# A two-layer attention trunk on one core: 464 instructions change places in a written-out order

## The chip, the cores and the metric

The kernel runs on one core of a Trainium2 chip. The time is that of the core on the device, in microseconds (us), from one execution to the next. A core has a matrix engine (TensorE, in the profile PE, with its weight loads as PEld), a vector engine (VectorE, DVE), a scalar engine (ScalarE, ACT), a general one (GpSimd, POOL) and a queue engine (SyncE, SP) that here issues nearly all DMA transfers. Each engine works through its own list of instructions in order, and waits at an instruction until what it needs is there.

## The reference, cut to what matters

Two layers over 1024 tokens of width 1024, with 256 context tokens; layer 0 is grouped-query attention with rotary positions, layer 1 neighbourhood attention with a bias. Both have a SiLU gate path, adaLN modulation ahead of the projection, and a gated residual.

```python
for i in range(DEPTH):                       # DEPTH = 2
    mod_x = (silu_c @ w_mod[i] + b_mod[i])[:, None, :]
    mod_c = silu_cc @ w_mod[i] + b_mod[i]
    hx = rms_norm(x, norm_g[i]) * (1.0 + sc_x) + sh_x
    hc = rms_norm(ctx, norm_g[i]) * (1.0 + sc_c) + sh_c
    if i % N_MIXERS == 0:
        yx, yc = gqa_axial_mixer(hx, hc, ...)      # 16 query heads, 4 key heads, 1280 keys
    else:
        yx, yc = neighbourhood_mixer(hx, hc, ...)  # 16 heads, 8 x 16 window and 256 context keys
    x = x + g_x * yx
    if not last:
        ctx = ctx + g_c * yc
return rms_norm(x, final_norm_g)
```

## The kernel before

The work is tiled by 128 tokens: 8 tiles of x, 2 of context. Matrices are multiplied as pairs of float16 parts (a high part and the rest), three matmuls for each product. The program has these stages:

- **Start** (0 to about 50 us). `mod_cols` computes the modulation of layer 0 from `w_m0`: for each of eight blocks kt two loads `wm{kt}0` and `wm{kt}1` (L780, 512 KB each), 16 matmuls into `pm` (L787), a copy `mrow` (L789) and small matmuls (L796) whose results become the scales `acol` and `scol`. `ln_pre` loads a tile of x into `xstage` (L1046, 512 KB), squares it on ACT (`xj`, L1049), takes the root (`ms_ln` L840 on DVE, `rs_ln` L842, a power on POOL), and scales it (L1052). `h_kt` transposes the scaled tile on PE into `pl` (L1061), from which ACT makes x's high part (L1066) and DVE the rest (L1068, L1071). `load_w` brings weights of the keys and values (`wskv`, L1026, 256 KB) and splits them (ACT L912, DVE L913). `kv_mm` multiplies (`pkv`, L1075). Ahead of all, 26 matmuls named `idle` (L1023) run on a tile of ones.
- **Layer 0** (about 50 to 700 us). For each of eight pairs of heads: projections `pa` (L1224), norms and rotary positions of the queries (DVE L986, L995), scores `st` (L1474), exponentials `pf` and `ph` (ACT L1461, L1459), the split of the probabilities (POOL L1326), products with the values `pv` (L1332 to L1336), and the eviction to `og` (ACT L1308, DVE L1310 to L1314). A part of the scores is computed in the other orientation (`qs`, `qpf`, `qpp`, `qpv`).
- **The seam** (about 700 to 765 us). The output projection `poa` and the residual (`x`, L1577 on POOL), the norm of layer 1 (`lss` L855, `ms_ln`, `rs_ln`, L859, L860), its split into `hrb` (ACT L871, DVE L872), and the first projections of layer 1.
- **Layer 1** (to the end). The projections of a pair of heads u, queries and keys in `b_qk`, values and gate in `b_vz`, are one Winograd-Strassen product each (`winograd`): seven block products (PE L1739 into `pwq{u}a` to `d`, L1787 into `pwv{u}a` to `d`) and sums on DVE (L1681 to L1700) between them. `b_load` loads weights into `wsb` (L1646), forms sums of them in `wtb` (POOL L1649 to L1651), and splits both into `wb` (ACT L1653, DVE L1654). `put_v` evicts values to `bv` (ACT L1768, DVE L1769), `put` evicts keys and queries to `bk` and `bq` (ACT L1726 to L1730, DVE L1727, L1731). Attention follows as in layer 0: scores `bsn` and `bsc` (L1820, L1821), maxima `bmx` and `bnx` (DVE L1839 to L1850), exponentials `bph` and `bpf` (ACT L1858 to L1861), transposes by DMA (L1864), values `bpv`. Last come the output projection `pob` (L1959) and the final norm.

What sets the order: the code above is first recorded in the order in which it is written. Then a table of numbers, `TABLE`, gives for each engine, ACT, DVE, PE, POOL and SP in turn, the order in which its recorded instructions are to stand: each entry is the step, less one, from the position of one instruction in the recording to that of the next. `settle` reads the table and `apply` lays it on the program. So each engine's list is an order written out by hand or by a search; at run time nothing is reordered. The waits between engines follow from the data, and from which buffer is reused: `bank`s of PSUM of each tag come in twos, so that the third user of a tag waits for the eviction of the first.

Where the new order puts a matmul later, it also puts its weight load (PEld) later. Where a step of `load_w` or `b_load` is moved, the loads that SP issues for it are rows of their own and may keep their place.

Of the kernel before, what the change touches and what calls it, by code (L numbers as in the profile page):

```python
# [61 lines left out]
y<TM?;?Uj`ke_eEIM4r(c9!O}n7Ew^`oV(p51ra716@KMo$P+=V@8?W-MX0ReVGo2!tQgy&C%5ApQASn2!F+z*T3J(z=)3mX?~?ARjZrTyMqjN<=r-
wkl_udfOGsQdA6c5Ioq9cBt?m#}T_=DCTT^FNpm;Bu`)xi8GPVLdEzWxG1I;8;hZZC!0*-}WO1Q_wS`t;;n7x@-KfvwcUqT-XlnJ7#X*a4NX51@kx856
szu#dXczI;S9R25~lQiPk}luN&kR*akD@96q-
7ctP1QGuLy@nog(<9TN!OR8iU0)`ib?LUS+{L@7&M*qCfP3a53X>h1Pi%gz>WSKDUjI$?W5f4e+7Hgo%I*QQy@_POr$Gq*2%bbpYb1H_T44;Q}g!GiKz
Q53VFw|1!isH|%X4II{e%nz4t|Hd;rsn<IMr9Ia>Th0Yj+vk7K&V{}Y93FlNpW}6l*vr;chYmIjLTX0OoKBcq=<1x)o*afy1iEnqw_)3M;s0mOPWZP%$
# [2013 lines left out]
```

## Time and profile before

| | us |
|---|---|
| three runs | 1301.15, 1302.62, 1303.58 |
| their median | 1302.62 |
| the profiled execution | 1301.96 |
| its span, first to last instruction | 1300.2 |

The page of the profile gives busy time by engine; the table of waits gives for each engine what it waited for and how long; the windows cut the span into stretches; the timeline shows single instructions as start, duration, engine, line, operation, output and inputs, with the idle time before it in brackets and what ended it. Line numbers are those of the kernel before.

### The profile page before, as it was taken

To read this page: it belongs to the slowest core of one execution; us is meant where nothing else is said; L and a number is where in the kernel's file an instruction comes from. 1 tells how busy PE (TensorE), PEld (TensorE's weight loads), DVE (VectorE), ACT (ScalarE), POOL (GpSimd) and SP (SyncE) were. 2 spreads that over 40 slices of the span, in tenths; PEclk is the share of its full clock that TensorE was granted. 3 is DMA by queue.
4 is the path that set the end of the run, shared out by engine and by line. 5 is a ranking of instruction groups with operands and counts; after the bars stand their busy time and mean duration, and the time that the engine had idled before them with its cause. 6 is when DMAs were issued, how large, how long until landed. Compare 5 with 4: busy or idle time off the path is not lost. (4 is left out here: it accounts for less than half of the span.)

```text
span 1300.2 us, 36307 instructions
## 1 busy us (share of the span) xinstructions
PE 1277.7 (98%) x13597; PEld 908.6 (70%) x13597; DVE 1049.0 (81%) x2625; ACT 1015.0 (78%) x2246; POOL 929.2 (71%) x1303
## 2 busy tenths in 40 slices
...
GB/s 364 217 153 84 120 140 148 156 180 155 157 170 156 168 157 148 132 180 188 101 114 192 218 124 87 145 157 143 146 148 158 142 154 147 157 151 204 315 149 113
DMA packets 446016, 209.32 MB, mean 161 GB/s; under 512 B 403280, under 2 KB 409616, under 8 KB 445840
## 3 DMA queue, kind: packets, MB, share of 16 engines
...
q8 instruction: 106, 1.74, 0.5%
...
## 5 line engine op out<-in xcount | busy, mean ns | idle before, releaser
L1326 POOL TENSOR_TENSOR pl<-pf,ph 128x256 f16<-128x256 f32 x322 | 222.7, 713 | 31.5 <-ACT pf L1461 25.4
L1326 POOL TENSOR_TENSOR bph<-bpf,bph 128x256 f16<-128x256 f32 (+1 forms) x224 | 181.2, 825 | 71.0 <-ACT bpf L1860 51.4
L1224 PE MATMUL pa<-wa,x 128*128 128x256 f16 x1536 | 228.3, 272 | 0.4 <-DVE q L1004 0.4
L1326 POOL TENSOR_TENSOR qpp<-qpf,qpp 128x256 f16<-128x256 f32 (+1 forms) x254 | 149.2, 607 | 40.3 <-ACT qpf L1416 29.2
L1787 PEld LDWEIGHTS <-hx 128*128 128x128 f16 x2688 | 162.4, 98 | 11.1 <-issue 3.7
L1224 PEld LDWEIGHTS <-x 128*128 128x128 f16 x1536 | 141.2, 97 | 35.3 <-issue 1.2
L1459 ACT ACTIVATE ph<-st 128x512 f16<-128x512 f32 x190 | 112.0, 598 | 26.5 <-PE st L1475 23.0
L1461 ACT ACTIVATE pf<-st 128x512 f32<-128x512 f32 x190 | 113.3, 603 | 0.5 <-POOL pl L1326 0.3
L1403 DVE CUSTOM_DVE_ANT_0 qpf<-qs,zero 128x512 f32<-128x512 f32 x156 | 92.8, 596 | 23.7 <-POOL qpp L1326 16.6
L1739 PEld LDWEIGHTS <-wb 128*128 128x128 f16 x672 | 63.0, 98 | 66.7 <-issue 2.3
L1415 ACT ACTIVATE qpp<-qpf,qnx 128x512 f16<-128x512 f32 x156 | 101.1, 654 | 9.1 <-DVE pa L990 1.7
L1259 DVE TENSOR_REDUCE mxp<-pm 128x1 f32<-128x512 f32 x152 | 101.5, 682 | 5.6 <-PE pm L1258 5.1
L1336 PE MATMUL pv<-v,pl 128*128 128x65 f16 x760 | 104.9, 193 | 0.0
L1416 ACT ACTIVATE qpf<-qpf,qnx 128x512 f32<-128x512 f32 x156 | 101.9, 653 | 1.9
L1858 ACT ACTIVATE bph<-bpf,bnx 128x384 f16<-128x384 f32 (+1 forms) x128 | 72.4, 584 | 32.7 <-DVE bnx L1850 24.5
L1332 PE MATMUL pv<-v,ph 128*128 128x130 f16 x570 | 89.3, 220 | 0.4 <-DVE og L1314 0.4
L1336 PEld LDWEIGHTS <-pl 128*128 128x128 f16 x760 | 70.5, 97 | 17.1 <-POOL pl L1326 1.6
L1959 PE MATMUL pob<-wob,obf 128*128 128x512 f16 x336 | 81.6, 379 | 0.0
L1649 POOL TENSOR_TENSOR wtb<-wsb 128x256 f32<-128x256 f32 x64 | 56.7, 886 | 25.5 <-DVE wb L1654 11.2
L1336 PE MATMUL bpv<-bv,bpht 128*128 128x65 f16 x608 | 74.8, 192 | 0.0
L1860 ACT ACTIVATE bpf<-bpf,bnx 128x384 f32<-128x384 f32 (+1 forms) x128 | 73.8, 583 | 0.6
L1474 PE MATMUL st<-q,k 128*128 128x512 f16 x190 | 71.1, 379 | 1.0 <-ACT pf L1461 0.8
...
## 6 DMA issues: line engine op xcount, KB each, us to landing
...
```

Source lines behind the costliest of these rows:

```text
L1224: T.matmul(ps[:, :, i, :], hA(a, kt, t), wt[w][:, kt, :], start=n == 0, stop=n == 3 * KT - 1)
L1259: V.tensor_reduce(mxs[i][:, t, ch:ch + 1], pm, axis=AX.X, op=ALU.max)
L1326: G.tensor_tensor(lo[:, c], p32[:, c], hi[:, c], op=ALU.subtract)
L1332: T.matmul(pv[:, c:c + 130], hi, v[:, 0:130], start=first, stop=False)
L1336: T.matmul(pv[:, c:c + 65], lo, v[:, 0:65], start=False, stop=last)
L1403: V.tensor_tensor_reduce(pf.rearrange("p a b -> p (a b)")[:, 0:n], st[:, 0:n], zero.broadcast_to([P, n]), op0=ALU.add, op1=ALU.max, scale=1.0,
L1415: S.activation(ph, pf, AF.Exp, bias=nmx)
L1416: S.activation(pf, pf, AF.Exp, bias=nmx, accum_out=sums[:, t, c:c + 1])
L1459: S.activation(ph, st, AF.Exp)
L1461: S.activation(p32, st, AF.Exp)
L1787: T.matmul(ps[:, t * P:(t + 1) * P], hx[a][:, t, blk, kt], wt[j][:, s_, w, kt], start=first and t == 0 and m == 0, stop=last and t == 3 an ...
L1959: T.matmul(ps, ob[kt][:, t, a], wout["b"][hf][b][:, kt, :], start=n == 0, stop=n == 3 * len(kts) - 1)
```

## The change

Only `TABLE` is another; every instruction and every wait's reason stays. Its first lines, cut:

```diff
-c-qBW31D1R)jn^TeKIrI*CuJ3wzQN2vO|kdz@jVyWm6DE1rbC9LHR{cT)<y`WJmoGl!Aclh%73IKou%2Ev1Dv-
...
+c-
+qZ;2Y_Q`wg0&#J(FZ6(`R<d?(8m$y9)wRcabVQDbhhfo+zLKN)eSO(k$SUM=zo%>Pi!kB2ttlMPa3Hf$ckOr|q;%GU>VB|D5mMo7|Sn48nW=J0;1zUp@
...
```

The new table takes two more lines of text, so each line of the code behind it has a number higher by two (L1769 becomes L1771). Counted as the fewest instructions that have to be taken out and put elsewhere to turn one order into the other, 100 of 13,261 matmuls, 154 of 2,625 operations on DVE, 98 on ACT, 52 on POOL and 60 of the loads and stores of SP change places, 464 together. Most go past one to four neighbours. Three places follow.

**DVE, values of pair 6** (trace: 1115.7 to 1120.6 us). `bv16` is the pair's values, `pwv6a` the first bank of their product, `wb700` the weights of the pair after it, `bq20` its queries. Before:

```order
L1848 TENSOR_REDUCE bnx506_20918<-bmx506_20868 128x2
L1654 SCALAR_TENSOR_TENSOR wb700_20790<-wsb701_20949,wb700_20790 128x3x128
L1850 TENSOR_SCALAR bnx506_20918<-bnx506_20918 128x1
L1727 SCALAR_TENSOR_TENSOR bq20_13049<-c12q6_20665,bq16_20274 64x4x128
L1769 TENSOR_TENSOR bv16_20276<-pwv6a_20673,bv16_20276 128x4x2x64
L1654 SCALAR_TENSOR_TENSOR wb700_20790<-wsb702_21077,wb700_20790 128x3x128
```

Now:

```order
L1850 TENSOR_REDUCE bnx506_20918<-bmx506_20868 128x2
L1656 SCALAR_TENSOR_TENSOR wb700_20790<-wsb701_20949,wb700_20790 128x3x128
L1771 TENSOR_TENSOR bv16_20276<-pwv6a_20673,bv16_20276 128x4x2x64
L1852 TENSOR_SCALAR bnx506_20918<-bnx506_20918 128x1
L1729 SCALAR_TENSOR_TENSOR bq20_13049<-c12q6_20665,bq16_20274 64x4x128
L1656 SCALAR_TENSOR_TENSOR wb700_20790<-wsb702_21077,wb700_20790 128x3x128
```

The subtraction of the values goes ahead of a small operation and of the product for the queries. On ACT the cast of `bv16` (L1768) goes at the same place ahead of the conversion of `wsb702` (L1653).

**PE, values of pair 0** (trace: 757 to 761 us). `wb011` is the weights, half made when the first two of these matmuls run; `pwq0b` is a bank of the product for the queries. Before:

```order
L1787 MATMUL pwv0d_13984<-wb011_13880,hx0_13039 128x128
L1787 LDWEIGHTS hx1_13040
L1787 MATMUL pwv0d_13984<-wb011_13880,hx1_13040 128x128
L1787 LDWEIGHTS hx0_13039
L1787 MATMUL pwv0d_13984<-wb011_13880,hx0_13039 128x128
L1739 LDWEIGHTS wb001_13597
L1739 MATMUL pwq0b_13755<-hx0_13039,wb001_13597 128x512
```

Now the third `pwv0d` stands nearer the end of the `pwq0b` group:

```order
L1741 MATMUL pwq0b_13755<-hx1_13040,wb001_13597 128x512
L1789 LDWEIGHTS hx0_13039
L1789 MATMUL pwv0d_13984<-wb011_13880,hx0_13039 128x128
L1741 LDWEIGHTS wb001_13597
L1741 MATMUL pwq0b_13755<-hx0_13039,wb001_13597 128x512
```

The third matmul into `pwv0d` has moved behind eight of the twelve into `pwq0b`. Beside it, ACT converts `wsb012` (L1653) directly ahead of `wtb011`, and POOL takes the power of the norm (L842) ahead of two sums of weights (L1649, L1651). DVE's rows ahead of the one for `wtb011` (L1654) change only among themselves.

**SP, the start** (trace: 0 to 20 us). The first twelve loads. Before:

```order
L780 DMA wm00_185<-in_w_m0 128x1024
L1046 DMA xstage0_105<-in_x 128x1024
L1026 DMA wskv0_189<-in_a_wkv 128x512
L780 DMA wm01_187<-in_w_m0 128x1024
L1046 DMA xstage1_106<-in_x 128x1024
L780 DMA wm10_202<-in_w_m0 128x1024
L780 DMA wm11_204<-in_w_m0 128x1024
L1046 DMA xstage2_107<-in_x 128x1024
L1046 DMA xstage3_108<-in_x 128x1024
L780 DMA wm20_282<-in_w_m0 128x1024
L1026 DMA wskv1_206<-in_a_wkv 128x512
L780 DMA wm21_284<-in_w_m0 128x1024
```

Now:

```order
L782 DMA wm00_185<-in_w_m0 128x1024
L1028 DMA wskv0_189<-in_a_wkv 128x512
L1048 DMA xstage0_105<-in_x 128x1024
L782 DMA wm01_187<-in_w_m0 128x1024
L782 DMA wm10_202<-in_w_m0 128x1024
L1048 DMA xstage1_106<-in_x 128x1024
L1048 DMA xstage2_107<-in_x 128x1024
L782 DMA wm11_204<-in_w_m0 128x1024
L782 DMA wm20_282<-in_w_m0 128x1024
L1048 DMA xstage3_108<-in_x 128x1024
L782 DMA wm21_284<-in_w_m0 128x1024
L1028 DMA wskv1_206<-in_a_wkv 128x512
```

Weights go ahead of tiles of x at two places, `xstage2` comes ahead of `wm11`, and `wskv1` goes behind `wm21`.

Two swaps more that the prediction speaks of: on DVE the queries' product L995 goes ahead of the eviction L1314 of `og22` (trace: 326.6 us), and on ACT an exponential into `pf` (L1461) goes ahead of one into `ph` (L1459) at 324 us. From 1195 us on, a dozen loads for the output projection (`obf`, `acc`, `wsob`, `fg`) and of the bias table `tb` change places in SP's list; PE's order of the last 60 us is the same in both.

More of the change, by code (lines that the diff above doesn't have):

```diff
@@ L62 @@
[L62 to L66, printed above, removed]
@@ new lines @@
+C80>Cbr5-h57R3xeWL;q71?hU;lQu5B%3ZDb)Y;I!%{<V=o#4onGB^-
+fP(0C(1%5^5&|*_X=rtA^x^C*#ctGPSLUQWm?yDS9$Q7OCL%f_EI5lTie>5{fI5RFH<MLsK}6p=MXsl~V*6M~9W`5?Q6WI~v15Wu?HhAVj<aYG1P8_V{
+B7^}SRWY!z^D0#(IXW$XKKMuIyROej8YCXMq-D{kx>yY#rH-0rQl#G3vVq!{R3O=MkJ!JTp`d0B$I2U22aN+p>)BY1N-
+BOw~kqPw7`K~&_pHyE!SBVN0+foVnXyE8N=uaI=f=w?Q%vqVXOrrF;?jmsICcjb~Zk&);aQ4l-
+u<!CI4AWnKrs8&2vR3}H=5`xpRQouJJ^ix6a7`m>UD<}HXk<sdOWCEv!G$o1(Rq^~-)Rk8>0vcwOn3nQ_(mEjL3X<f?r9DU@l-
+68IXqpz>Q#dgJ2^g6~Vu2<Vg3lYv$s|ox>BtC9%ST=Lr#<P~NkJl^4s5Ff7-|B&D-
@@ new lines @@
+$OZ*F2i2QmQAz<3bpR`mcp`qtSmXsDE`~Zp)GlpKf0dOa64n6DZl(HMqAXKZUe`y>|Bdz|-325)fVVUUqM9I}S$@d<l>A-
+cKHylu!@@ZzH&>dv*7Bm#x`9kqDsPzq29{K)4ysPA^^`ocAF%xd_n+OrQWg^|j&rWQ~9rf23|?*_xJW_i!wT`rX|L{&d0j{_<%*p~NJF)2T4P>qm$v&A
+kEw)!}-
+1o6A>?bA`wx?1HRB4AkBodbbnmhf%CH?>8dWjMa?6`sI10Wk=|>J?s0GpxfL3?(XmI{+{y8Ezj&5jfJwVuipyeZ9RzP&%f@nlTO}>l{>cA;gm^}tEN!@
+QF{>%2p)H=dokVv?}zPN-
+4A;e(jUNXYXI`g4=DU|?Ky8iUdl%&(Qu*4r}vmZ$e*eoMy1V?AsDWQj=>aE#hV8dRMLc87?~H6`+|uYj5koI1tY)_c;JAROK=sWv}+=oapzGvUHL?9hW
+wa|;EanvP-fcinh-*06q5iRsQ?8Rf|~%kvD{S6SR<qbZywMHde9W7d=hqoz9N+L4>ZRSR`BwI)V9GbK%3G_Zaa|R-
@@ new lines @@
+tvNLB*bDkMEo_E206qgii6mD&y<&fe72z=Gm9Y+>ea1i+9>ZG)LX|qwQK-THBd8~EAHZo3oJL?4{}KXtNhOL`0Dg`CzoOTI>ZkGba{xQ>rCKXPs1TB?;
+lP(+PhVL!zKoAozOvH!;cNJ}FU;-
+|%x^3oMW?5R|IhkXT8h9^pI2X>J%Zd`()R=$s?8nXiDOBUD8PmLR?LHkP6iBvA3POr{1HwA70cqa>dRCL3!@=;lmHfxga-
+0N9Pq<?U49SV3%e0BA=guYahs|QWam(Mv8y<WRc%}&sE8jiPMdB)R)-PO2>xk&*EBuZ<l>{ry$zp*$-
+x$~sKmJG2yE^muCyjglk0(Y91OpX`pYQ*AHXg+L4dXJDSq=0{QqeWK-V7I$7&XHH2*8Sb2h-
++d!QbJ_`;s+_KQK)6v_}zW1zLKF%8*JEySmu)p|LoF<!f~7PcYM1R#{r+72XD02l7tYGB%LH4*wH|9=)NDJ(b%-
+&|Yx5V~X(+@@|6S<0H><Z9q&0N?#N75uK5rz$5d*4|$SJo>=?C=rAVF<*bjzaOG$q^u=YyG6VGb(&`&5#@A~>G#%e(fu2>X2lb<g7@PvzK8rh9^d~7N&
@@ new lines @@
+MRj9GeJ4pd|l;;G2iKI2hc^(K!JuhCfr<H>I_+8@vb0-{-JFNNe}@MTb~)0T<jB;hyRI2lGc-NEL;v0Tyi}YHkT#h}NJ^d(c;8kFFEjb;iA;-
+B=1YUzh`lI5Pw{e2=SG)t%qOI-?Jq_S!L`#ssLp;si9fS8C+=n^yY`>KUnhP47H-
+^b&mcJlRTk21nSu19e5X1HNfA5jVm`+JH33gN6=U5Tn}X9pE)Vr*FY6--eq>21(Wta}c8D4gekhks)}@^@f2COW`PZHp>~X@@X!%n`oe|CSv`Mg?OZWy
+Z+{j+NYWtD$p@VJp=K1ikjUzAKq(6*`j#0et65mO;|*R{o#F0oYg4_=fRzzTK4}&>-l4`G;z^pENMoRbk^_fd>#(LmqvuD^}6+*(vxk5x-
+n8Mu?1Nh;U@KK_vq9*?H-
+l0gu>8uc#nP(M8sF*Vq+XB?fKSV=lz!1H|mwqhM~N4?)&$WY1bHmLtMBCNxvAiF1>UU&?`Oi77Y}IKO`o3G>gjtehPpg_?f73-
@@ new lines @@
+m5*E*tc^3)j+&7Q%Xz;xTnuhC+e8;9n?XkpmG3is;~<6yaESTqeVhG)ZIZxn+SH40!ZutvQ73LQZ>Mzy{lpK`E6NID}J43>U587__?D2^jpL^QT4h)j(
+SKB~`kli*LmL-
+@XMjqi_ic>xJk7(3pxmu#OQT63MD!x0hX~n~IC!w|rvW^Wir9_)UxowCg;|M93)Df6%?qHLGBg4mlCq{{lyS)*Y&WAWc|!_HRT>_;@@8a<Jrps;7;UI7
+o=Vrf7o}4{P|mMW3PO|C^!z5bf4_1GfJrMO;40-
+J(0X7;Y%xef|0h=&^D)CnRkXKv4G`3nkH({QgXQz2~gADS+q|l+h9hdj8PoKWCCDGWbaMyaYF>wkbLqg)wr+wFsQAxsrtbD*VwQ?N@$ajhdvwH}AakXA
+)fUX8;W{c;Q?M&t*g<y1_aDG|86vqOJI~Uw`e_>Zl}LY%<a*e^kXsy@{pNF@B07dhgq4=ihHu`z2F^-
+5viZ!b0_047BF5aMQwVTq3ZFUx))GD@B7NKAQadqi|e=2)`UoanPv;;NdU9UzN4Gny4??VNr*cqH3Bc6GrL42};Zpp8Cwcc-
@@ new lines @@
+CaT}aZM*8?BH3^9jbDbvUr}2WG@Fa)#C;^K%xK_Lh=*9OJFSl^<yYMekG<0R3f69CCi>99D@eql4usi}U9i%0STKbEX(U!b<;v*+=Fx0ab#=VqmpHKJS
+nMcsreEm)j!qU2n`Kx~fzChjG8#tP~2=Buuy}Xx(tX@2r%gQglfvEB@E$Q{-
+ao1l8e>wqfJBORef1)RB{SSKZUss_Mz6I@X%TeSzMKyi!^K&WI7&aQUpM4*0B}u;a5<ZOIz_)pp=f?tEe$AD9Tq}<V#4pv&Ga(lc_gsx2pR!`RuZ90U?
+_}8h3jO&JB8j}~+rgh`dB&92rEbFd>ie*aPublGk`5gZ%53A3x(~cXDp<OXTuWK7wXjaN#^5rs{iTBdUVwwAt3X|-
+c=<pg(P7UWR&*mtEU4~kDCMpUUM9&=K<Sej1lRCwaCwxVVZA4AY$U!-X2zu#-
+W*S_V&F9E#Tt7#^9_|{v_PYZRCLsUyr>}UIT_N^V5%M9*SPuf1cWQ}`H`=NQd)HB+NGuYt9g27xb(AhxZE#3HMUqaW&bfu%X~#9oPSEtbapEv=4+^-
@@ new lines @@
+hSGjG<SIrni#9GY&cZ72q;InBTzFJVJN;&VEn8!Z3bp3tmsBGSd#|SbAwn^VrImiY>;d`+(7s5I9Y=HTgsmcqc1iPo@qk#WK#Cz-c%P#sYn3&-
+uPwUBB<v3E36n7Q8U2p7Yo^;6<AyDM(zb&BvB8QN3Y5g_Ktv$n-
+Z{wrc(sO<hoHEZgH+(cn`zzQTerdmw_RYW(5BO1wYi~PW@W3jMR!`|vSMu7psxn$<%DUoX|Zp12&4p=y5N((cD3Dk&EOE!>z`Vl^c5@oaD!&3p>rb+c5
+5*<tlfL{?ZzDb6NdH=1t$cO18J$A!r!IGK&q1T)~nk{fV-
+1)Nz#|7iJ39J%o{8ER86XlxY}$G>P7@D%H{h&!jm?AFnVVBBjD;vQtcEi7M&rK@jp)2>|}bbS5*m7*L<9~`mG9*XC<F8`8QiLMLT9x1OjT%Uqm3UtVH?
+M*1Y!y@gMuV!NW;zyWiYP%XbzNAQCNJ(%EIYo$P?moLPK$2;ZFn@Rwo^Mu&|@=Lkd=ZME)>6NE&UN__mIJjFR>fC7GixS?adHBnR-R%+G#-
@@ new lines @@
+-6iXG*Hw#Gt7<GFTR}NfgobyV6M+|W~^eF;A|1nJ`M_r1{_jU#e^Ta}<_)baG;%uj~u5dm>`-
+j~y&_TN#)#^1sqJ_0^@F3w3&>Rykat$@`>fq;YCx%cSNjDim*A#{KYl$O5bc9&VQ|@8`<wx*J0uDn`+$2Y0(#KccT}lF6qA$(2x{w*qW&-
+$JO*9GuDFuB2Q*qb2z`x5xq9eyzRzTm=E-
+DJ0wUsjNlt4MUpA?1V``2^1bDw{E7S3FiQ@$FW3eR)BCBq(HJL8bm7^z70@9o=D;3svDlK(8H;KavH{!^ZBwxnL@yr?HZbHaB%PY;r*c2vp-
+(s@6fXFcY*BVRdGehkB{L<qctVUl=nZ!H~6^5xMo2d8Ph#FZ6}e>QW%gMQx;H?*GifUHRJxDO>L?j4H2xZjOjjiw<y$j_(CjlJ+C&+otb$RwO|T`l-
+izAT7tB{%J_qEp76^jM96VllB`6#81hl?x<5icEWA5Z>AzKk*Ui#23<OkiYO`;rPc3;$%3I%%HWX&(%%xEJydUxLANt^%s6QfU;SYPl0&O1DP{dVIODS
@@ new lines @@
+E1<cYY?`J7u>f+eac~H+tc)nvKOIbBNGIbPd7v#%-
+&7Jv?(#1m$o?sR>jn`PY+Tfn>DmIp%y<KA+IL4z^iFh9+I3*M8q(>u%y>02o<QF8>9jSaySJsk!?m#m`W8(~;GYy+zA2X?_>n9q$4WIMQ|?Rz_>nw1te
+#%IQV>Kzo)W6!C<neI1o9~)1DY-
+oyiy_<7pvl8Ad&J3iCX=k5K8!x!9=DeF5++@Rg<KLNOkWxGM66aB2*I}@|v_aO-$gUK*~2I`BMJr{zXZ&;~sGon+;&RAb9gxAt1)|KB-whKJ<+QN`2z9
+aTf%VLX9v6sU~4eAp3=^3kXx;hE0Vq8NpcCo0+H&ZK+KPp)tQ_65Rem%1z&#vbjDK3yR9d#bTkqMNk8afhPO*492uq{-
+gf#clulHm8t*u6Rn6=m1)J9_5k#9dPBvwS+T6C7i(9B@i5DMeGJ9EjO~{`fd0rh5Mxiq31}lL4WiV%)}202R%(`&`ZLZ+8@#0@W||M^jWYAi64~^c`e2
@@ new lines @@
+!P2KuOt6~HuS)1;Y!xt38BTeono*uPqUnLd{$XCk5XnOP#Vj*3JniJgfArt-
+!qFryGzCufwGBDah}V`OHD^Cq&IXlLuc$VMy6OfqQdwWu;y;+O_*WGNUcfN_+@Uq`Z7=W38p>j#UfS!Zn^g-M4@*1~v8FAugG799j@4;D5-
+Q9?`#!fcc-mSI+A8pT5ImzfoSnR;awK{BYKQAMnyU|_e9rPdr+Z4^BdNz5u~lu~2khCAAgqGDPsXi4x&3Rsd~JAI8E0CO@U4&ua&BXdx9lg=C1YH$`{V
+HVhUXcJX48*NGe%wC@{W|S(+tc(NH{%nF^(hHND0LxHqdSuk<qR@gx0*o%yqWT7-
+W0oP4Y#54JsAjW~R^M(>S!Sk`%@&p@YSa*;#8|0h5<s(NSk1hhEOtdTdnAM0ltuzZvtsh|%+4W$3%6KgqhNx`c9rg$AOtg^949AaGUqn0rWdf*w;?hcf
+HBkDU>Hr9LMI|)7PrD!xtTKnJJW0q55VFN9aYw7t&OmXl}2D7tO+jKZMh=`U}jn|=IDZ$-
@@ new lines @@
+K`b*#|%R=NH}A*X_@9>^epBs%_?gkF*BJ{g9Ub`BxAPmTg-
+!XWG0Jkwv9%3Ye5zolPn@<aUTW)3U;1bzzQ&%7ctV$NDPyCGzASd;8Vt=81XY>cBpG~_9lC30TEV&Vz%vOi)G}b2|t_TB$LT9sH`K-
+H5w%oJxn@dvKU|rA56Z<Xd}Q3Cu}-x!aQK(g2hQ13?sA29$4|HH4?J`EsGB@$0EiN+apLP18<T>qr{q~#jH`38H+ez8D_=TR-A3MT2>-
+k+_WXywTXf$&a_w%d%OXrc*AO<tzON79c>O1zyVJ)u)sC2Fw`1*8<9V=%)y8um=&~u2?bjrx{>x~&uWP|Y*CD1oMt=CEFrK_j~!zi=Zk>_H?T@!k`X<c
+DqA`SE8cakz%0N9?0Cj_zlagcFp*hoIG7<WV-~uY`~<V-
+AuQbiSTxNvSLOufoPi#5w$k>e%vy%A8TiSdLJ0={TNf*T%VbF^&7MI8dOA^wIsCKp%|sttKF=7sm?9J#C@ZHo%#vrY#6e&inkCw?1c46e23D5P%zBp@r
```

274 lines of the change are left out of this document (106 added, 168 removed).

## The prediction

> **What bounds the kernel.** I read the page first, then the table of waits of TensorE (PE), then the windows, and last the timeline of each engine at the places that the change touches. The page:
>
> ```profile
> span 1300.2 us, 36307 instructions
> PE 1277.7 (98%) x13597; PEld 908.6 (70%) x13597; DVE 1049.0 (81%) x2625; ACT 1015.0 (78%) x2246; POOL 929.2 (71%) x1303
> ```
>
> PE works 1277.7 of 1300.2 us. The change adds and removes no instruction, so this work stays. What an order can win is PE's idle time, 1300.2 - 1277.7 = 22.5 us, and part of that is the launch and the tail after the last matmul. The waits of PE on other engines, longest first, 12 of the 28 rows (columns: what waited, for whom; us in total, times, longest):
>
> ```profile
> PE pkv L1075 <- ACT x L1066: 1.7, 2, 1.1
> PE idle L1023 <- DVE zero L740: 1.5, 1, 1.5
> PE pwv6c L1787 <- DVE bv L1769: 1.2, 1, 1.2
> PE pwv0d L1787 <- ACT wb L1653: 1.1, 1, 1.1
> PE pl L1061 <- DVE ms_ln L840: 0.9, 1, 0.9
> PE st L1474 <- ACT pf L1461: 0.8, 2, 0.5
> ...
> PE pwv0c L1787 <- DVE wb L1654: 0.6, 1, 0.6
> ...
> PE pv L1332 <- DVE og L1314: 0.4, 1, 0.4
> PE pm L787 <- DVE s L755: 0.4, 1, 0.4
> ...
> PE pwq0c L1739 <- DVE c22q L1695: 0.2, 1, 0.2
> ...
> PE pv L1332 <- ACT ph L1459: 0.2, 1, 0.2
> ```
>
> All 28 rows add up to 14.4 us (those not shown have 0.2 to 0.7 each). The 1.5 us ahead of the first matmul are set by the launch; 12.9 us are left. Two stretches that the argument needs (columns: window, PE busy, PEld, DVE, ACT, POOL, granted clock, DMA share, GB/s):
>
> ```profile
> 1100.00:1150.00 50.00, 48.53 (x668) 40.04 (x666) 43.30 (x108) 42.53 (x93) 40.22 (x54) 1.00 0.71 144
> 1200.00:1250.00 50.00, 50.00 (x361) 27.26 (x359) 28.65 (x78) 25.32 (x57) 31.21 (x36) 1.00 0.98 251
> ```
>
> From 1200 us on PE is full: what the change moves there, a dozen loads among it, can win nothing. I follow four places, and bound the rest.
>
> **Place 1, the values of pair 6 (1114 to 1121 us).**
>
> ```profile
> 1118.14 0.78 PE L1787 MATMUL pwv6b<-wb,hx 128*128 128x128 f16 x11
> 1120.08 0.72 PE L1787 MATMUL pwv6c<-wb,hx 128*128 128x128 f16 x10 [1.16 <-DVE bv L1769]
> 1117.38 0.56 DVE L1654 SCALAR_TENSOR_TENSOR wb<-wsb,wb 128x384 f16<-128x384 f32 x1 [0.84 <-ACT wb L1653]
> 1118.04 1.26 DVE L1727 SCALAR_TENSOR_TENSOR bq<-c12q,bq 64x512 f16<-64x512 f32 x1
> 1119.33 0.69 DVE L1769 TENSOR_TENSOR bv<-pwv6a,bv 128x512 f16<-128x512 f32 x1
> 1117.26 0.56 ACT L1768 CAST bv<-pwv6a 128x512 f16<-128x512 f32 x1
> ```
>
> The subtraction L1769 frees pwv6a's bank, which pwv6c takes. It stands behind a product for the queries, L1727, which takes 1.26 us and which PE doesn't want yet. After the change L1769 comes first, right behind the weight row of 1117.38, and ACT casts bv (1117.26) before one of the weight conversions (L1653) that stood ahead of it. The cast then ends by 1117.8 at the latest, the weight row by 1117.94, and L1769 by 1117.94 + 0.69 = 1118.6. PE ends its last pwv6b at 1118.92, so the wait of 1.16 is gone with 0.3 us to spare. I count **-1.2**. Behind it L1727 ends about 0.3 later (0.69 moved ahead of it, less what DVE waited for ACT), and no PE row near it asks for it. What is late next is the next wait of this stretch:
>
> ```profile
> 1139.20 0.69 DVE L1846 TENSOR_REDUCE bmx<-bsc 128x2 f32<-128x512 f32 x1 [0.90 <-PE bsc L1821]
> 1143.59 0.27 PE L1820 MATMUL bsn<-bk,bq 128*128 128x256 f16 x1 [0.32 <-DVE bmx L1839]
> ```
>
> At 1143.59 PE waits for DVE again; but DVE itself had waited 0.90 us for PE at 1139.20, so it starts earlier when PE does, and the gain passes through. Bounds: 0 (all given back there) to -1.3 (the start of pwv6c against the end of pwv6b's last, 1120.08 - 1118.92 = 1.16, and the drain of that matmul).
>
> **Place 2, the values of pair 0 (747 to 765 us).**
>
> ```profile
> 758.33 0.22 PE L1787 MATMUL pwv0d<-wb,hx 128*128 128x128 f16 x1 [1.11 <-ACT wb L1653]
> 758.39 2.75 PE L1739 MATMUL pwq0b<-hx,wb 128*128 128x512 f16 x12
> 762.97 0.33 PE L1787 MATMUL pwv0c<-wb,hx 128*128 128x128 f16 x3 [0.58 <-DVE wb L1654]
> 751.84 0.15 DVE L840 TENSOR_SCALAR ms_ln<-lssb 128x1 f32<-128x1 f32 x1 [0.67 <-ACT hrb L855]
> 753.30 1.21 DVE L859 SCALAR_TENSOR_TENSOR x<-x,rs_ln,lrow 128x512 f32<-128x512 f32 x1
> 757.62 0.76 DVE L859 SCALAR_TENSOR_TENSOR x<-x,rs_ln,lrow 128x512 f32<-128x512 f32 x1
> 762.24 1.28 DVE L1654 SCALAR_TENSOR_TENSOR wb<-wtb,wb 128x512 f16<-128x512 f32 x2
> ```
>
> One pwv0d matmul waits 1.11 us for a weight row. It goes behind eight of the twelve pwq0b matmuls, 8 x 2.75 / 12 = 1.8 us of work, and the row has come by then, even with one conversion (0.5 us) put ahead of it on ACT. So that wait goes. But PE then comes to the wait at 762.97 1.1 us sooner, and the row it wants is made by DVE at 762.24, at the end of a run that began at 751.84 and has no idle time; the change leaves the same work ahead of that row. The 0.58 becomes about 1.7. Sum here: **0**, bounds -1.1 (if DVE's run shortens as much) to +0.5 (if one of its rows lengthens). Rows of it can: the same operation L859 took 1.21 us at 753.30 beside POOL's weight sums and 0.76 at 757.62. [...]
>
> **Place 3, the start (0 to 21 us).**
>
> ```profile
> 10.91 1.06 ACT L1049 ACTIVATE xj<-xstage 128x1024 bf16<-128x1024 f32 x1 [1.63 <-DMA xstage<-in_x]
> 14.76 1.06 ACT L1049 ACTIVATE xj<-xstage 128x1024 bf16<-128x1024 f32 x1 [2.07 <-DMA xstage<-in_x]
> 18.36 0.75 DVE L1052 TENSOR_SCALAR xstage<-xstage,rs_ln 128x1024 f32<-128x1024 f32 x1 [0.40 <-POOL rs_ln L842]
> 18.42 1.94 PE L787 MATMUL pm<-wm,s 128*32 128x256 f32 x16
> 20.29 1.33 PE L1061 MATMUL pl<-idf,xstage 128*128 128x128 f32 x5
> ```
>
> Twelve loads (wm and xstage 512 KB, wskv 256 KB) go through SP's queue one after the other. xstage1 landed at 10.91 and xstage2 at 14.76, with three 512 KB loads from the one to the other: 3.85 / 1.5 MB = 2.57 us per MB. In the new order xstage0 has 0.25 MB more ahead of it (+0.64 us), xstage1 0.5 MB more (+1.3), xstage2 0.5 MB less (-1.3), xstage3 0.5 MB more (+1.3), wm21 0.25 MB less (-0.64). The waits of the start (pkv 1.7, pl 0.9, pm 0.4: 3.0 us) change among themselves. What counts is when PE reaches the run that begins at 18.42 and no longer stops: pm there needs wm21, the five pl at 20.29 need xstage3. If wm21 decides, -0.6. xstage3 was scaled by 18.36 + 0.75 = 19.11, 1.2 us ahead of the five pl, which covers nearly all of its 1.3; without that cover it costs +1.3. I take **-0.2**: wm21's gain, less what xstage1 and xstage3 may show of theirs; bounds -0.6 to +1.3.
>
> [...] The stretch has the lowest granted clock of the run:
>
> ```profile
> 8.00:21.00 13.00, 9.35 (x73) 3.87 (x72) 8.73 (x27) 6.60 (x15) 2.88 (x6) 0.89 1.03 409
> ```
>
> [...]
>
> **Place 4, two swaps at 324 to 327 us.**
>
> ```profile
> 324.43 0.38 PE L1474 MATMUL st<-q,k 128*128 128x512 f16 x1 [0.28 <-ACT pf L1461]
> 326.88 0.23 PE L1332 MATMUL pv<-v,ph 128*128 128x130 f16 x1 [0.38 <-DVE og L1314]
> 326.55 0.28 DVE L1314 TENSOR_TENSOR og<-pv,sz 128x128 f32<-128x128 f32 x1
> 326.75 0.42 DVE L995 TENSOR_TENSOR pa<-pa,gq 128x256 f32<-128x256 f32 x1
> ```
>
> ACT's pf comes ahead of another exponential, so 0.28 goes; but DVE now puts L995 (0.42) ahead of L1314, for which PE waits: +0.4. Together **+0.1**, bounds -0.3 to +0.4.
>
> **The rest.** Of the 12.9 us the places hold 1.2 + (1.1 + 0.6 + 0.2) + 3.0 + (0.3 + 0.4) = 6.8; some 6.1 us stand in waits of 0.2 to 0.5. Some 400 moves of one to four positions fall among them. At three of the longest of them (one each of qpv, st and pwv2c) the rows of the producer keep their order, and a producer that comes forward elsewhere pushes back the row it passes. I take a sixth, **-1.0**; bounds -3.0 (half) to +2 (five new waits like place 4's).
>
> **Sum:** -1.2 + 0 - 0.2 + 0.1 - 1.0 = -2.3. The profiled execution took 1301.96 us, so 1299.7; the median of the runs is 1302.62, 0.66 above it, so **1300.3**.
>
> **Rivals.**
> - *The waits go widely.* Place 2's second wait and the start give their bounds too (-1.1 and -0.6), and half the rest goes: -1.2 - 1.1 - 0.6 + 0.1 - 3.0 = -5.8, 1296.8. For it: nearly every long wait of the table has its producer moved. Against: DVE's run at 751.84 without idle time.
> - *Given back.* Place 1's gain ends at 1143.59, the rest cancels: about 1302.6. For it: PE already waits there.
> - *Slower: something pushed ahead of a row PE waits for,* as L995 ahead of L1314. Each costs some 0.4 us. To be 0.2% slower (2.6 us), with -1.2 from place 1, it takes (2.6 + 1.2) / 0.4 = 10 such places; eleven give 1305.8. 464 moved instructions leave room for that; that only one of the longer waits shows it speaks against.
> - *The clock at the start.* xstage0 and xstage1 come later, and the stretch of 13 us loses as much clock again, 0.11 x 13.0 = 1.4 us, on top of +1.3 for the place: -2.3 + 1.4 + 1.5 = +0.6, 1303.2. [...]
>
> **How the numbers follow.** Forecast 45%, with a range of its own of 1298.4 to 1302.2; waits go widely 24%; given back 16%; slower 11%; clock 4%. The range takes in the forecast, most of the second case and of the third, and the costs' bounds: **1296.6 to 1304.4**. A measurement of this kernel tells 0.2%, 2.6 us, from no change; the forecast lies just inside. Two fifths of its cases are faster by more: 18 + 24 = 42% faster, 27 + 16 + 3 = 46% the same, 12% slower.
>
> **What would show it.** Right: no wait for bv at pwv6c, PE busy near 49.7 in 1100 to 1150; pwv0d without a wait and pwv0c with about 1.7; the join of the start at 20.1; a new or longer wait for og near 326. Wrong: pwv0c's wait unchanged (place 2 then pays), the five pl later than 20.3, a table of waits whose total has not fallen below 13, or many new rows with L1316, L1656 or L1841 as releasers.

## The result and the profile after

| | before | changed |
|---|---|---|
| median of 13 runs | 1303.58 us (1300.06 to 1305.36) | 1307.00 us (1303.33 to 1308.85) |
| ratio | 1 | 1.0027, 95% interval 1.0016 to 1.0038 |
| profiled execution | 1301.96 us, span 1300.2 | 1308.51 us, span 1306.7 |

The changed kernel is slower, by 3.4 us of median to median. Its profiled execution is 1.5 us above its own median, and that of the kernel before 1.6 us below its own, so the two profiles differ by 6.5 us: what they show below is nearly twice what the runs lose. From its page, the lines of span, busy time and granted clock (40 equal slices of the span, in tenths):

```profile
span 1306.7 us, 36313 instructions
PE 1284.4 (98%) x13597; PEld 910.3 (70%) x13597; DVE 1051.8 (80%) x2625; ACT 1012.8 (78%) x2246; POOL 923.3 (71%) x1303
PEclk7999999999999999999999999999999999999999
```

The last of these lines in the kernel before:

```profile
PEclk9999999999999999999999999999999999999999
```

PE's busy time grew by 1284.4 - 1277.7 = 6.7 us, as much as the span (6.5), although PE does the same matmuls. So they ran longer: in the first slice the clock is down. The trace's record of the clock has it at half for 13.65 us from 13.54 us on, and for 3.41 us from 767.88 us on; in the kernel before only for 3.41 us, from 18.16 us on (the tail behind the last matmuls left out). By an estimate that takes PE as working all that time, half the difference, (13.65 + 3.41 - 3.41) / 2 = 6.8 us, is the growth of PE's busy time in this pair of profiles. The waits of PE in the changed kernel, 20 rows that add up to 14.0 us, against 14.4 before:

```profile
PE pm L798 <- DMA sel<-in_sel_c: 2.2, 1, 2.2
PE qpv L1427 <- DMA qpp<-qpp: 1.7, 1, 1.7
...
PE pwv0c L1789 <- DVE wb L1656: 1.3, 1, 1.3
PE pkv L1077 <- ACT x L1068: 1.1, 1, 1.1
PE pwv2c L1789 <- DVE bv L1771: 0.9, 1, 0.9
...
PE pwv3b L1789 <- DVE w1v L1683: 0.5, 1, 0.5
...
PE pv L1334 <- DVE og L1316: 0.2, 1, 0.2
```

The rows for pwv6c and pwv0d, 1.2 and 1.1 us before, are gone; a row for `sel` has come first that no table before had. To see where time is won and lost I set each matmul's start in the changed profile against its start in the profile before:

| stretch of the profile before | change of the lag in it, us |
|---|---|
| 0 to 23 us | +4.9 |
| 300 to 577 | -2.0 |
| 577 to 618 | +2.3 |
| 746 to 766 (place 2) | +0.4 (-2.1, 1.1 of it the wait of pwv0d; then +0.8 at pwv0c and +1.7 by the clock) |
| 780 to 1000 | +3.4 |
| 1000 to 1010 | -0.8 |
| 1120 (place 1) | -1.3 |
| end | lag 6.5 |

The start first. `sel` is a small constant that the matmuls L796 multiply with. In the kernel before, ACT issues its load among its first instructions (ACTq is ACT's queue of DMA issues; start, duration):

```profile
2.14 0.50 ACTq L758 DMA_DIRECT2D sel<-in_sel_c  x1
```

In the changed kernel, ACT's and PE's timeline at the same place (line numbers higher by two):

```profile
2.13 1.28 ACT L750 ACT_TABLE_LOAD   x1 [2.13 <-issue]
7.67 0.22 ACT L750 ACTIVATE cth<-cct 128x16 f32<-128x16 f32 x1 [4.25 <-DMA cct<-in_cc]
7.68 0.33 ACTq L760 DMA_DIRECT2D sel<-in_sel_c  x1
13.70 0.99 PE L798 MATMUL pm<-sel,mrow 128*128 128x2 f32 x4 [2.17 <-DMA sel<-in_sel_c]
24.54 1.33 PE L1063 MATMUL pl<-idf,xstage 128*128 128x128 f32 x5
```

ACT's `cth` went ahead of the issue of `sel`. `cth` waits for `cct`, which lands at 7.67, and the issue of `sel` waits behind it: 7.68 instead of 2.14. `sel` lands 6.0 us after its issue, PE waits 2.17 us for it, and the run of five pl starts at 24.54 instead of 20.29. The windows of 3 us show what came of PE's idle time (columns as in the tables of windows above: window, length, PE busy, PEld, DVE, ACT, POOL, granted clock, DMA share, GB/s). Changed, then before:

```profile
12.00:15.00 3.00, 0.99 (x4) 0.93 (x4) 0.28 (x3) 1.15 (x2) 0.00 (x0) 0.76 1.04 406
15.00:18.00 3.00, 2.20 (x14) 0.73 (x18) 2.15 (x7) 1.49 (x3) 1.05 (x1) 0.50 1.02 400
18.00:21.00 3.00, 2.71 (x15) 1.16 (x7) 1.60 (x6) 1.49 (x3) 0.55 (x1) 0.50 1.04 404
21.00:24.00 3.00, 2.58 (x19) 0.95 (x19) 2.20 (x7) 0.97 (x2) 0.55 (x1) 0.50 1.04 408
24.00:27.00 3.00, 3.00 (x17) 1.57 (x10) 1.41 (x4) 1.54 (x3) 0.00 (x0) 0.50 1.02 400
27.00:30.00 3.00, 3.00 (x20) 1.90 (x18) 2.34 (x6) 0.76 (x3) 0.00 (x0) 0.97 1.03 404
```

```profile
15.00:18.00 3.00, 1.45 (x8) 0.87 (x8) 1.86 (x8) 2.35 (x6) 0.77 (x2) 1.00 1.03 398
18.00:21.00 3.00, 3.00 (x22) 1.15 (x21) 2.30 (x5) 1.12 (x3) 0.33 (x1) 0.53 1.04 408
21.00:24.00 3.00, 3.00 (x20) 2.13 (x19) 1.94 (x5) 2.19 (x4) 0.00 (x0) 0.91 1.03 403
```

The clock falls in the window in which PE works 0.99 of 3 us, and is at half for 13.65 us; before, it falls behind the one with 1.45 of 3, for 3.41 us. No single wait of PE here is longer than 2.2 us. That PE's idle time is what halves the clock is a guess at this point, which `e5_fill` tests.

### The profile page after: what moved, and what is told of

Same layout as the page of the kernel before. It is cut to its first block, busy times and chain, and to the rows that moved or that the text cites. A ratio compares the mean times of both kernels' runs of the same rounds, so it can differ in the third digit from the quotient of the medians.

```text
span 1306.7 us, 36313 instructions
## 1 busy us (share of the span) xinstructions
PE 1284.4 (98%) x13597; PEld 910.3 (70%) x13597; DVE 1051.8 (80%) x2625; ACT 1012.8 (78%) x2246; POOL 923.3 (71%) x1303
## 5 line engine op out<-in xcount | busy, mean ns | idle before, releaser
L1461 ACT ACTIVATE ph<-st 128x512 f16<-128x512 f32 x190 | 112.3, 598 | 27.4 <-PE st L1477 23.5
L1405 DVE CUSTOM_DVE_ANT_0 qpf<-qs,zero 128x512 f32<-128x512 f32 x156 | 92.8, 595 | 23.4 <-POOL qpp L1328 15.5
L1651 POOL TENSOR_TENSOR wtb<-wsb 128x256 f32<-128x256 f32 x64 | 55.2, 864 | 28.0 <-DVE wb L1656 14.4
L1427 PE MATMUL qpv<-v,qpp 128*128 128x128 f16 x520 | 71.3, 219 | 2.4 <-DMA qpp<-qpp 1.7
```

The lines of the kernel that those rows point to most:

```text
L1405: V.tensor_tensor_reduce(pf.rearrange("p a b -> p (a b)")[:, 0:n], st[:, 0:n], zero.broadcast_to([P, n]), op0=ALU.add, op1=ALU.max, scale=1.0,
L1461: S.activation(ph, st, AF.Exp)
```

## The experiments

Each kernel below takes a part of the two orders; but for the added matmuls of `e5`, nothing else differs. Each was timed beside the kernel before on the same chip, and its ratio is to that; the groups ran on five chips. In the diffs the rows have the line numbers of the kernel before.

### Is it the late load, or SP's new order of the first loads?

`e1_sel_back`, the changed kernel but for one row of ACT:

```diff
+L758 DMA sel_87<-in_sel_c 128x2
 L748 ACTIVATE cth_79<-cct_77 128x16
-L758 DMA sel_87<-in_sel_c 128x2
 L1049 ACTIVATE xj0_177,xss0_178<-xstage0_105 128x1024
```

> The changed kernel with one thing undone: ACT issues the load of sel ahead of cth again, as before. Theory (late sel): PE no longer waits for sel at L796, the run of five pl (L1061) starts at 20.3 +- 0.7 instead of 24.5, the granted clock is halved for 2 us at most in the first 30 us, and the time falls by about 4.8 us below the changed kernel: ratio to before 0.9990 +- 0.0010. Rival (the order of SP's first twelve loads): the five pl still start after 23, ratio 1.0027.

Measured: ratio 1.0010 (0.9999 to 1.0021), the five pl at 21.28, both a little above what was expected. By this the late load is worth 0.0017 of the 0.0027, some 2.2 us; the 4.8 were too much to expect, as the profiled execution had drawn a long stretch of half clock. 0.0010 is left without it. The intervals of 1.0027 and 1.0010 overlap, so this step alone doesn't prove the price.

`e2_sel_only`, the kernel before with `cth` ahead of the load of `sel` and of the first `xj`, as in the changed kernel (`e1` leaves `cth` ahead of `xj`):

```diff
-L758 DMA sel_87<-in_sel_c 128x2
-L1049 ACTIVATE xj0_177,xss0_178<-xstage0_105 128x1024
 L748 ACTIVATE cth_79<-cct_77 128x16
+L758 DMA sel_87<-in_sel_c 128x2
+L1049 ACTIVATE xj0_177,xss0_178<-xstage0_105 128x1024
```

> The kernel before with one thing of the change: on ACT cth goes first, then the load of sel, then the first xj. Theory (late sel): PE waits some 2 us for sel, the five pl start at 24 to 25, clock 0.50 for about 10 us, ratio to before 1.0035. Rival (SP's loads): five pl at 20.3, ratio 1.0000.

Measured: 1.0018 (1.0004 to 1.0031), PE waits 2.4 us for `sel`, the five pl at 23.55:

```profile
14.65 0.98 PE L796 MATMUL pm<-sel,mrow 128*128 128x2 f32 x4 [2.35 <-DMA sel<-in_sel_c]
23.55 0.82 PE L1061 MATMUL pl<-idf,xstage 128*128 128x128 f32 x5
```

The same from the other side, half as much as the 1.0035 expected: the clock is at half for 6.83 us in this profile, not 10.

`e3_first_loads`, the kernel before with the twelve rows of SP shown in the change:

```diff
 moves of the change that are kept
-ACT 98, DVE 154, PE 100, POOL 52, SP 60
+SP: the first twelve loads
```

> The kernel before with the change's order of SP's first twelve loads alone. Theory (late sel): the five pl start between 19.6 and 21.6, ratio within 0.9995 to 1.0010. Rival (SP's loads): the five pl start after 23, ratio 1.0035.

Measured: 0.9996 (0.9986 to 1.0006), the five pl at 20.45, as the theory had it. The rival falls.

### Wait or clock?

`e5_fill` keeps `sel` late, and gives PE ten more matmuls on ones to do while it waits; what they compute is not used.

```diff
-    for n in range(26):
-        T.matmul(idle, ones[:, 0:P], ones, start=n == 0, stop=n == 25)
+    for n in range(36):
+        T.matmul(idle, ones[:, 0:P], ones, start=n == 0, stop=n == 35)
```

The ten stand in PE's order behind the first transpose into pl, ahead of the first matmul with `sel`.

> The changed kernel with ten more of the matmuls on ones (2.2 us of work, their result unused as that of the others) put ahead of the matmuls that wait for sel, so that PE is busy while sel is late. If the halved clock is a consequence of the idle time: clock 1.0 until 16 us, the five pl at 22 to 23 (sel's own lateness of 2.2 us stays), ratio 1.0010. If the clock has another cause: clock 0.5 from 14 us as before, five pl at 24.5 or later, ratio 1.0027 or more.

Its windows:

```profile
12.00:15.00 3.00, 2.79 (x15) 1.45 (x15) 0.50 (x2) 1.15 (x2) 0.00 (x0) 1.00 1.03 398
15.00:18.00 3.00, 2.07 (x20) 0.76 (x20) 2.52 (x9) 1.69 (x4) 1.05 (x1) 1.00 1.03 405
18.00:21.00 3.00, 2.07 (x17) 1.08 (x20) 2.11 (x9) 2.03 (x5) 1.10 (x2) 1.00 1.03 403
```

The clock stays at 1.00 and the five pl start at 21.88: of the 4.25 us by which they were late, 2.7 were the clock's in this pair of profiles. Of the 20 profiles this is the only one in which the clock doesn't fall at the start. It holds beyond one draw: the granted clock over a whole execution is 0.9980 in the mean of `e5`'s 12 executions, 0.9950 in 13 of the changed kernel and in 12 of `e2`, and 0.9968 in 35 of the kernel before. By an estimate from these means the late `sel` costs 0.0018 x 1303 = 2.3 us through the clock, which is about all that it costs. That the wait of 2.2 us itself is made up again behind it is argued from this, not shown.

More work made this place faster, but the kernel hardly: the ratio is 1.0016 (1.0005 to 1.0027), where 1.0010 was expected, and its interval overlaps that of 1.0027. The ten matmuls are 2.2 us of work themselves.

### The gains: places 1 and 2

`e6_values`, the kernel before with the compute engines' moves at 747 to 766 and 1113 to 1121 us (5 rows on ACT, 6 on DVE, 2 on PE, 1 on POOL, counted as in the change):

```diff
 moves of the change that are kept
-ACT 98, DVE 154, PE 100, POOL 52, SP 60
+ACT, DVE, PE, POOL: 747 to 766 us, 1113 to 1121 us
```

> The kernel before with the change's moves of ACT, DVE, PE and POOL at 747 to 766 us and at 1113 to 1121 us alone. Place 1: no wait for bv at pwv6c, PE 1.2 us earlier from there to the end. Place 2: pwv0d without a wait, pwv0c waits 1.0 to 1.7, PE 0.3 to 0.7 earlier behind it unless the clock falls after that wait. In all -1.5 to -1.9 us, ratio 0.9987. Rival (both gains are given back later): ratio 1.0000 and the offset at 1290 us within 0.3.

Measured: 0.9987 (0.9976 to 0.9999), as expected. In its profile PE comes 1.3 us earlier at pwv6c and stays so to the end. At place 2 PE wins 1.10 at pwv0d and gives 0.76 back at pwv0c; then the clock drops. PE's timeline there:

```profile
764.97 0.33 PE L1787 MATMUL pwv0c<-wb,hx 128*128 128x128 f16 x3 [1.34 <-DVE wb L1654]
766.17 3.35 PE L1739 MATMUL pwq0c<-hx,wb 128*128 128x512 f16 x8 [0.21 <-DVE c22q L1695]
```

and the window of 3 us behind them (columns as in the table of the start):

```profile
768.00:771.00 3.00, 3.00 (x18) 1.50 (x17) 2.97 (x5) 1.99 (x4) 1.61 (x2) 0.69 0.20 42
```

The trace has the clock at half from 766.42 us on for 3.41 us; there the matmuls into pwq0c follow one another every 0.43 us, at the full clock every 0.22. The changed kernel's own profile shows the same, the seven others with place 2's moves (`e1`, `e5`, `e8` to `e11`, `e19`) do not, with waits of 1.0 to 1.3 us there. The steps of the clock lie 3.41 us or whole multiples of it apart in each trace (in the changed one at 13.54, 27.19, 767.88 and 771.30 us). In the 3.41 us ahead of the fall PE worked 1.75 us, in both profiles; in `e8`, where the clock did not fall, the stretch with the wait in it has 2.09 (759.60 to 763.01 us, by an estimate that carries the steps at its start on in multiples of 3.41). So with waits of 1.0 to 1.34 us the clock fell in two of nine profiles; what decides in which was not shown.

### The losses elsewhere: SP's moves, or the compute engines'?

`e7_queue` tried the two places where SP's moves seemed to explain a loss:

```diff
 moves of the change that are kept
-ACT 98, DVE 154, PE 100, POOL 52, SP 60
+SP: 553 to 574 us, 910 to 924 us
```

> The kernel before with SP's moves at 553 to 574 us and at 910 to 924 us alone (a load of wg, loads of wsoa and of wsb against transposes of qpp and bph). Theory (queue): PE waits about 1.7 for qpp at 579 us, and ACT waits for the transpose of bph near 916, PE 1 us later by 920; together +2.5, ratio 1.0019. Rival (these losses come from the compute engines' moves or from the draw of the transfers): offset within 0.5 at 900 us and at 1000, ratio 1.0000.

Measured: 0.9990 (0.9981 to 1.0000). The theory fell: neither loss appears with SP's moves alone. `e8_no_queue` takes all compute moves, without SP and without the late `sel` (ACT has `sel`, the first `xj` and `cth` in their old order):

```diff
 moves of the change that are kept
-ACT 98, DVE 154, PE 100, POOL 52, SP 60
+ACT 96, DVE 154, PE 100, POOL 52
```

> The changed kernel without SP's 60 moves and without ACT's late sel: the 400 moves on PE, DVE, ACT and POOL alone. If the losses are sel's and the queue's: -1.2 (place 1) -0.6 (place 2) and -0.5 elsewhere, ratio 0.9982. If the compute moves lose as much in the middle as they win at the two places (884 to 1000 us, +3): ratio 1.0005 to 1.0010.

Measured: 0.9981 (0.9968 to 0.9993). The compute moves make the kernel faster. Its profile has the late wait for qpp at 579 us too (1.13 us, against 1.7), so most of that loss comes with the compute moves alone. `e9_part` keeps those of them where the profiles showed gains:

```diff
 moves of the change that are kept
-ACT 98, DVE 154, PE 100, POOL 52, SP 60
+ACT, DVE, PE, POOL: 300 to 560, 740 to 766, 1000 to 1010, 1113 to 1121 us
```

> The kernel before with the compute engines' moves at 300 to 560, 740 to 766, 1000 to 1010 and 1113 to 1121 us, where the changed kernel gained on the kernel before in both profiles. If these gains are the moves': -1.2 -0.6 -1.0, ratio 0.9979. If those at 300 to 560 are the draw of the transfers: ratio 0.9987, as for the values alone.

Measured: 0.9960 (0.9944 to 0.9976), better than the 0.9979 expected, and faster than both kernels; the waits of PE in its profile add up to 10.2 us, 4.2 fewer than before. What wins more than the three gains counted on is not shown. The same without place 2 is `e13_part_less`:

```diff
 moves that are kept, against e9_part
-ACT, DVE, PE, POOL: 300 to 560, 740 to 766, 1000 to 1010, 1113 to 1121 us
+ACT, DVE, PE, POOL: 300 to 560, 1000 to 1010, 1113 to 1121 us
```

> The compute engines' moves at 300 to 560, 1000 to 1010 and 1113 to 1121 us alone: the kernel that gave 0.9960 without place 2. If place 2 pays: 0.9965, some 0.3 to 0.7 us slower than that one. If the clock that fell behind place 2's longer wait in two profiles of five costs more than the place wins: 0.9955.

Measured: 0.9960 (0.9948 to 0.9972). Place 2 is worth nothing that can be told.

Then SP's moves by halves, beside all compute moves. `e10_queue_late` and `e11_queue_early`:

```diff
 moves kept besides ACT 96, DVE 154, PE 100, POOL 52
-SP 60
+SP: from 590 us on
```

> All the change's moves on PE, DVE, ACT and POOL (sel in its old place), and SP's from 590 us on. The moves without SP gave 0.9981, with all of SP's 1.0010. Theory (SP's later moves cost): 1.0000 to 1.0010, with a loss of some 1.5 us at 884 to 950 us and one near 1206. Theory (SP's early moves cost): 0.9981.

```diff
 moves kept besides ACT 96, DVE 154, PE 100, POOL 52
-SP 60
+SP: ahead of 590 us
```

> The same with SP's moves ahead of 590 us instead. Theory (SP's early moves cost): 1.0000 to 1.0010, with losses near 316 and 433 and at 579 us. Theory (SP's later moves cost): 0.9981. If both halves cost, each gives 0.9990 to 1.0000.

Measured: 1.0001 (0.9989 to 1.0013) and 0.9996 (0.9983 to 1.0009), against 0.9981 without SP's and 1.0010 with all: either half seems to take away part of the gain, though the intervals overlap. `e12_middle` takes all engines' moves in the stretch of 3 us lost:

```diff
 moves of the change that are kept
-ACT 98, DVE 154, PE 100, POOL 52, SP 60
+ACT, DVE, PE, POOL, SP: 770 to 1000 us
```

> The kernel before with all of the change's moves, SP's among them, at 770 to 1000 us alone. The changed kernel and the one with sel put back both lost 3 us there in their profiles, the one without SP's moves 1.1. Theory (SP's and DVE's moves together make the waits at pwq3b, pwv3b and pwv4a): ratio 1.0015 to 1.0025, offset +2 to +3 at 1000 us. Theory (the lateness came from the draw of the transfers): ratio 1.0000 to 1.0008, offset below 1.

Measured: 1.0005 (0.9991 to 1.0020), which decides nothing; its profile loses 2.4 us from 770 to 997 us, as the first theory has it, and wins 0.6 back by 1012. `e14_queue_only`, `e15_other_part` and `e16_first_300` take the pieces alone:

```diff
 moves of the change that are kept
-ACT 98, DVE 154, PE 100, POOL 52, SP 60
+SP 60
```

> The kernel before with SP's 60 moves alone. If the moves of SP's queue cost by themselves: 1.0025 to 1.0030. If they cost only beside the compute engines' moves, or by chance: 1.0000 to 1.0010.

```diff
 moves kept, against e8_no_queue
-ACT 96, DVE 154, PE 100, POOL 52
+the same without those of e9_part
```

> The kernel before with the compute engines' moves outside of 300 to 560, 740 to 766, 1000 to 1010 and 1113 to 1121 us (and sel in its old place). If the moves add up: 0.9981 - 0.9960 = 0.0021 lost, ratio 1.0021. If the 0.9981 of all of them is only place 1, place 2 and the draw: 1.0000.

```diff
 moves kept, against e8_no_queue
-ACT 96, DVE 154, PE 100, POOL 52
+those of them ahead of 300 us
```

> The kernel before with the compute engines' moves ahead of 300 us alone. If these lose what the profile of all the compute moves showed by 232 us: +2 us, ratio 1.0016, with the run of five pl some 0.8 us later than before and losses near 52 and 73 us. If that was the draw: 1.0000.

Measured: 1.0026 (1.0014 to 1.0038), 1.0009 (0.9998 to 1.0020), 1.0007 (0.9995 to 1.0018). SP's 60 moves cost by themselves, for a reason that the next run shows; the rest of the compute moves may cost a little, which these intervals don't settle.

### One swap in SP's list

In `e14`'s profile one place stood out. `e17_one_swap` makes that swap alone in the kernel before:

```diff
-L1646 DMA wsb201_15054<-in_b_wp 128x512
 L1864 DMA_TRANSPOSE bpht
+L1646 DMA wsb201_15054<-in_b_wp 128x512
```

> The kernel before with one swap in SP's list: a load of wsb goes behind a transpose of bph that stood after it (802 to 805 us). Theory (this swap is the costly one of SP's moves): POOL waits about 5 us for wsb at 810, PE 2 to 3 us for bpht between 815 and 825, ratio 1.0020. Rival (SP's moves cost a little in many places): PE's wait there below 1 us, ratio 1.0000 to 1.0007.

Measured: 1.0028 (1.0019 to 1.0037), one row of 60. SP, POOL and PE in its profile:

```profile
805.37 0.65 SPq L1646 DMA_DIRECT2D wsb<-in_b_wp  x1
809.76 0.73 POOL L1649 TENSOR_TENSOR wtb<-wsb 128x256 f32<-128x256 f32 x1 [5.42 <-DMA wsb<-in_b_wp]
824.50 0.23 PE L1332 MATMUL bpv<-bv,bpht 128*128 128x130 f16 x1 [2.08 <-DMA bpht<-bph]
```

The same load and sum in the kernel before:

```profile
802.38 0.33 SPq L1646 DMA_DIRECT2D wsb<-in_b_wp  x1
...
805.20 0.72 POOL L1649 TENSOR_TENSOR wtb<-wsb 128x256 f32<-128x256 f32 x1
```

The transpose is not ready when its turn comes, so the load goes out 3 us later; POOL stands 5.4 us at L1649, and behind it in POOL's list are the sums of bph that the next transposes need. These then come late, and PE waits 1.1 and 2.1 us for bpht.

But the swap is not what the changed kernel suffers from: in its profile POOL waits for no wsb there. POOL's own rows at 800 to 804 us are moved with it; that this is why is not shown. `e18_queue_but_one` and `e19_two_undone`:

```diff
 moves of the change that are kept
-SP 60
+SP: all but the swap of wsb201
```

> The kernel before with SP's other moves. Theory (one swap): 1.0005. Rival (many places): 1.0020 to 1.0026.

```diff
 moves of the change that are undone
+ACT: sel and the first xj ahead of cth
+SP: the swap of wsb201
```

> The changed kernel with the late sel and that swap undone. Theory (one swap): 1.0027 - 0.0018 - 0.0020 = 0.9989. Rival (many places): as with sel alone undone, 1.0010.

Measured: 0.9991 (0.9981 to 1.0001) and 1.0012 (1.0002 to 1.0022). SP's other moves alone cost nothing; in the changed kernel, undoing the swap wins nothing. So alone SP's moves cost through that one swap, and beside the compute engines' moves it is the others that cost. One place shows this cleanly. In `e19`'s profile, and in the kernel before:

```profile
944.77 1.83 PE L1787 MATMUL pwv3b<-wb,hx 128*128 128x128 f16 x30 [0.47 <-DVE w1v L1681]
```

```profile
942.90 1.28 PE L1787 MATMUL pwv3b<-wb,hx 128*128 128x128 f16 x20
```

This wait, about 0.5 us, is in the six profiles that have both the compute moves and SP's later moves at this place (the changed kernel, `e1`, `e5`, `e10`, `e12`, `e19`) and in none of those that have one of the two (`e7`, `e8`, `e11`, `e14`, `e15`, `e18`). A second place is like it: from 916 to 925 us PE loses 0.7 to 1.0 us in the changed kernel, `e1`, `e10` and `e19`, and 2.5 in `e5`, but 0.2 in `e12` and nothing in those six. A part of it is a wait that those five profiles have and no other; from `e19`'s table of waits:

```profile
PE pwq3b L1739 <- DVE w1q L1681: 0.4, 1, 0.4
```

## Why the prediction was wrong, point by point

- **What bounds the kernel: right in kind.** PE stays the bound and its idle time is all that an order can win. Its other half was missing: this order also lost, through the clock, more than the waits show. The waits add up to 14.0 us against 14.4, and PE's busy time grew by 6.7 and the span by 6.5. Of the prediction's own signs of being wrong two came: the five pl at 24.54 instead of 20.3, and a total of waits that had not fallen below 13.
- **Place 1: right.** Forecast -1.2, with L1771 done by 1118.6 in the times of the profile before; measured -1.3 in the changed profile, no wait at pwv6c, and kept to the end:

```profile
1126.69 0.83 PE L1789 MATMUL pwv6c<-wb,hx 128*128 128x128 f16 x12
1125.41 0.69 DVE L1771 TENSOR_TENSOR bv<-pwv6a,bv 128x512 f16<-128x512 f32 x1
```

- **Place 2: the mechanism right, its price incomplete.** pwv0d waits no more, and pwv0c waits longer, 1.34 for a forecast 1.7. Net -0.3 in the profiles instead of 0, and nothing that the runs can tell (`e9` against `e13`). What the prediction did not weigh is the clock behind the longer wait: it fell to half for 3.41 us in the changed profile and in `e6`'s, +1.7 us, and in none of the seven others. Of its two rows of L859, 1.21 and 0.76 us, both stood beside a sum of POOL, not the first alone: POOL's row had 0.65 us left at 753.30 and 0.21 at 757.62, 0.44 us between them, against 0.45 between the two of DVE. That POOL's row is what made the first one longer was not shown.
- **Place 3, the start: here the prediction failed.** It worked out -0.2 from SP's queue, and for SP's twelve loads alone that holds (0.9996). But it counted only SP's moves and says nothing of ACT's list there, where `cth` goes ahead of a DMA issue: `sel` is issued from ACT's own queue and went out behind `cth`, at 7.68 us instead of 2.14. The late `sel` costs 0.0017 to 0.0018, some 2.3 us, against the -0.2. The rival of the clock at the start, given 4%, named the mechanism with another trigger (xstage) and a smaller price: 1.4 us of clock, where the means over all executions give 2.3 and the pair of profiles with `e5` 2.7.
- **Place 4: half borne out.** The wait for pf at 324 us is gone, as forecast; the one for og that was to grow by 0.4 is down to 0.08 (the 0.2 for og in its table stands elsewhere, at 327.06 us). In the changed profile PE waits 0.26 us for another row (qmx, L1405) just ahead of that place, at 331.45 us, and so comes there later.
- **The rest: wrong in sign for the change as a whole, right for a part.** Forecast -1.0. The compute moves without SP's, places 1 and 2 among them, gave 0.9981, that is -2.5 us for a forecast of -2.1 without the start. That this is near is in part luck: the moves of four stretches alone gave 0.9960, so the gain did not come as a sixth of the waits everywhere. What took it away are SP's 60 moves beside them, 1.0010 - 0.9981 = 0.0029, or 3.8 us. This is the larger of the two terms that failed, and the prediction had no term for it: it bounded the queue's moves by the rows of PE's waits and followed only the first twelve of them and those behind 1195 us.
- **Sum of the parts as measured.** 0.9981 for the compute moves, +0.0029 for SP's moves beside them, +0.0017 for the late `sel`: 1.0027. These are steps from one kernel to the next, so that they end at the ratio measured is no test of them, and the middle one has an interval of about 0.0016 to either side. The test is in the runs from another side: `sel` alone gave 1.0018, and `e19`, which has 59 of SP's moves more than `e8` and differs in nothing else, 1.0012 against 0.9981.
- **Open.** Which of SP's moves, beside which compute moves, cost the 0.0029. The two halves seem to share it, one swap that is costly alone is harmless here, and two places (916 to 925 us and the wait at pwv3b, in most profiles 1.2 to 1.5 us of the 3.8 together) are tied to the meeting of two sets; why the two sets make them late was not taken apart further, nor was the rest.
